# Later places in a state space branch's step loop, and other step rates, in a two-layer decoder trunk

## Chip, core and metric

The kernel runs on one core of one Trainium2 chip. The metric is device microseconds of one execution. A core has TensorE (PE, with its weight loads as PEld), VectorE (DVE), ScalarE (ACT), GpSimd (POOL) and SyncE (SP). Each works through its own row of instructions in the order in which they stand there. SP holds no arithmetic; its row is a queue of DMA issues.

## The reference, cut to what matters

A prompt of 2048 positions and a sample of 8x4 go through two layers of width 1024. Layer 0 is `proj = x @ w_in`, split into `u` (768), a gate (768), a memory query and a memory gate (256 each). Its mixer is a diagonal state space model (S5) of 48 groups with 16 channels and 64 complex states:

```
bu = einsum(ug, b_bar)                  # inputs of the states
h  = associative_scan(a*h + bu)         # over 2048 positions
y  = real(einsum(h, c)) + d_skip * ug
y  = gelu(y);  y = y * sigmoid(y @ w_glu + b_glu)      # the GLU
```

Beside it four heads attend from the memory query to 256 memory tokens. Both branches are gated, joined and projected by `w_out`, and a layer norm follows. Layer 1 (dilated attention) is untouched by the change.

## The kernel before

**Layer 0 in two streams.** The main stream is `run_units` (L228): weight columns of 128 times 1024 (or 1056) positions, in blocks of 512, 256 or 288 columns. Each block is 8 steps over the inner dimension, and each step three fp32r products (`mm3`, L128 to L130: high by high, low by high, high by low). So a block is 24 products into a PSUM tile `mm`, of which there are three. A block's end is taken out by ACT and DVE: for gate blocks ACT L290 (tanh) and then DVE L291, and a DMA stores `s` (L294). For every unit of weights ACT splits off the high part `wh` (L123) and DVE the low part `wl` (L124). When the units pass from the second half of the positions to the first, `XH` and `XL` are made anew from `xraw` in the same way.

**The side stream** is a Python generator. `tick` (L96) is called after every step of a block with that step's product time. It adds time x `self.rate` to a sum, and for each whole unit the generator does one more step. The rates stand in `self.R` (L73): `R[0]` for the first units, `R[1]` for the memory queries and gates of layer 0, `R[7]` for its memory attention, `R[2]` during the GLU.

**The S5 branch** (`s5`, L732) is that side stream. It works on 12 slices of four groups. For slice q a loop of 13 steps does:
- `tab_use` of q+1: products `aux` (L560) of tables `BS` and `E`, taken out by ACT as `kev` (L563) and stored in `d_kt`; then transposes of table `F` (L575), taken out by ACT as `I` (L577);
- `s5_out` of q-1: two steps, each with ten products `y` (L702 to L706; two of them read `H`, the states, and `E`), ACT's `Y` (L708), a POOL copy and two DMA stores (L712);
- `s5_scan` of q: DVE operations on `V` (L647 to L650), `C`, `f` (L682 to L684) and `H` (L688);
- `s5_load_t` of q+1: four DMAs that read `T` back from `d_kt` (L611);
- `s5_in` of q+1: eight products `v` (L627) from `U` and `I`, taken out by ACT as `V` (L630);
- `tab_make` of q+2: POOL makes `BA`, `BB`, `BS` from `bcraw` (loaded at L492), and DVE makes `F` and `E` (L507 to L511) and the small `CA`, `CB` (L546, L547).

`T`, `V`, `H` and `I` have two buffers each, `E` and `U` three, `CA` one; `aux` and `v` have one PSUM tile each, and so has a pair of `y`. A new writer waits for the last reader of its buffer.

**What sets the order.** The text's order is not yet the order on the engines. The program is built with `schedule_with_timeline_sim=True` (L2190): the builder places instructions by an estimate of its own of when operands are ready. Each engine then runs its row as placed.

After the S5 branch, memory attention (L901) is the side stream, first under the last gate blocks, then under the GLU (L1121), which begins when the last y is stored.

Of the kernel before, what the change touches and what calls it, by code (L numbers as in the profile page):

```python
# [48 lines left out]
class Tiles:  # L49


    def __init__(self, at):
        self.at = at
# [6 lines left out]
class Trunk:  # L60
    def __init__(self, tc, ins, outs):
        self.tc, self.nc, self.i, self.o = tc, tc.nc, ins, outs
        self.turn = 0
        self.bg = self.cache_copies()
        self.side, self.rate, self.acc = None, 0.0, 0.0
        self.bgrate, self.bgacc = 0.0, 0.0
        self.done = set()
        self.primed = None
        self.q2 = tc.nc.gpsimd

        self.B = (0.16, 0.0, 0.35, 0.056)

        self.R = (0.8, 0.9, 0.307, 0.34, 0.44, 0.51, 0.54, 0.48)  # L73

    def pool(self, name, bufs=1, space=None, side=None):
        kw = {"reuse_waits": "tile"}
# [655 lines left out]
    def s5(self, keep, d):  # L732

        nc = self.nc
        self.E, self.I, self.U, self.T, self.V, self.H = {}, {}, {}, {}, {}, {}
        self.F, self.BS, self.TR = {}, {}, {}
        with self.pool("tab", side="right") as tab, self.pool("aux", space=PSUM, side="right") as aux:
            self.ZR = tab.tile([128, 48], F32, name="ZR")
            self.ZI = tab.tile([128, 48], F32, name="ZI")
            self.ZRS = tab.tile([128, 48], F32, name="ZRS")  # L740
            self.ZIS = tab.tile([128, 48], F32, name="ZIS")
            for _ in range(12):
                yield
            with self.pool("base", side="right") as base:
                yield from self.s5_base(keep, tab, base)
            self.s5_setup(tab, d)
            self.tab_load(tab, 0)
            self.tab_load(tab, 1)
            yield
            yield from self.tab_make(tab, 0)  # L750
            yield
            yield from self.tab_use(tab, aux, 0, d)
            yield from self.tab_make(tab, 1)
            self.tab_load(tab, 2)
            yield from self.wait("u0")
            with self.pool("s5", side="right") as pool, self.pool("s5ps", space=PSUM, side="right") as psum:
                self.s5_load(pool, 0, d)
                self.s5_load_t(pool, 0, d)
                nc.sync.dma_start(self.H0S, self.i["h0_stack"])
                yield  # L760
                self.s5_in(pool, psum, 0)
                yield
                for q in range(NSL):


                    if q + 1 < NSL:
                        yield from self.wait(f"u{(q + 1) // 2}")
                    self.s5_load(pool, q + 1, d)
                    use = self.tab_use(tab, aux, q + 1, d)
                    make = self.tab_make(tab, q + 2)  # L770
                    out = self.s5_out(pool, psum, q - 1, d) if q else iter(())
                    scan = self.s5_scan(pool, q)
                    for n in range(13):
                        if n in (0, 3, 4):
                            next(use, None)
                        if n in (1, 2):
                            next(out, None)
                        if n < 9:
                            next(scan, None)
                        if n == 5:  # L780
                            self.s5_load_t(pool, q + 1, d)
                        if n == 9:
                            self.s5_in(pool, psum, q + 1)
                        if n >= 5 and n != 6:
                            next(make, None)
                        if n < 10 or q + 2 < NSL:
                            yield
                    self.tab_load(tab, q + 3)
                yield from self.s5_out(pool, psum, NSL - 1, d)
                self.s5_finish(pool, d)  # L790
# [1422 lines left out]
```

## Time and profile before

| | us |
|---|---|
| median of 3 runs | 1975.45 |
| lowest, highest | 1974.0, 1977.9 |
| the profiled execution, its own time | 1975.58 |
| its span, first to last instruction | 1973.8 |

The profiled execution's time is 1.78 us more than its span. The S5 branch runs from about 130 to 430 us of the span, memory attention of layer 0 from 479, the GLU from 552 to 700. Matmuls are pipelined: one of 512 columns shows 0.39 us, but they start 0.23 us apart, so PE is shown busy also where it just keeps pace; where it shows idle time it has certainly run dry.

### The profile page before, as it was taken

Reading aid. Unit: us, or ns where it says so; the run is one execution under the profiler, and the core shown is the slowest. Engines: PE = TensorE matmul, PEld = TensorE weight load, DVE = VectorE, ACT = ScalarE, POOL = GpSimd, SP = SyncE. Lnnn points to the kernel's source line nnn. Section 1 sums busy time; section 2 is a strip of 40 time slices with the busy share of each in tenths; the row PEclk is TensorE's granted clock in tenths of the full one; section 3 lists DMA queues with packets and bytes.
Section 4 is the critical chain, followed back from the end, with each engine's and each line's share of the span. In section 5 each row is a group of like instructions: output and inputs, shape, how many; then the busy total and the mean of one; then the engine's idle time right before and its main releaser. Section 6 shows DMA issues by size and latency. Waiting matters only on the chain.

```text
span 1973.8 us, 35795 instructions
## 1 busy us (share of the span) xinstructions
PE 1926.5 (98%) x13446; PEld 1643.7 (83%) x13446; DVE 1178.9 (60%) x2766; ACT 686.9 (35%) x1585; POOL 425.9 (22%) x754
## 2 busy tenths in 40 slices
PE   8999999899989999999999999999999999999998
PEld 6789888788779988787898879899888877887777
DVE  8649989885575756667456326532652245345685
ACT  5343222333453421115445226532652246221110
POOL 0414444313332012210000020003103210412220
PEclk9999999999999999999999999999999999999999
DMA  7685556656367899988533266536547736768941
GB/s 227 180 249 135 163 171 190 206 184 221 109 174 224 237 309 345 359 277 261 169 122 109 83 219 201 147 84 211 184 129 227 243 113 177 236 195 260 292 176 75
DMA packets 371893, 388.44 MB, mean 197 GB/s; under 512 B 76104, under 2 KB 314104, under 8 KB 369208
## 3 DMA queue, kind: packets, MB, share of 16 engines
q1 hardware_dynamic: 344904, 257.52, 43.7%
q0 software_dynamic: 26816, 128.63, 19.4%
q8 instruction: 106, 1.74, 0.4%
q14 instruction: 67, 0.55, 0.1%
HBM read 280.30 MB, written 150.27 MB: 218 GB/s over the span
## 4 chain that ended last, share of the span: by engine, by line
PE 83%; DMA 7%; DVE 5%; issue 1%; SPq 1%; ACT 1%; POOL 1%; DVEq 0%; ACTq 0%; POOLq 0%
PE mm L128 22%; PE mm L129 22%; PE mm L130 22%; PE s L1034 4%; PE o L1657 2%; PE tp L1642 2%; PE o L976 2%; PE tp L963 1%; DMA wraw<-in_w_in 1%; DMA bcraw<-in_ssm_bc 1%; DMA kv<-in_c_v 1%; PE tp L1389 1%; DVE wl L124 1%; DMA craw<-d_cm 1%; PE v L627 1%
## 5 line engine op out<-in xcount | busy, mean ns | idle before, releaser
L128 PE MATMUL mm<-XH,wh 128*128 128x512 f32 (+2 forms) x1520 | 546.7, 360 | 12.3 <-ACT wh L123 7.9
L129 PE MATMUL mm<-XH,wl 128*128 128x512 f32 (+2 forms) x1520 | 539.4, 355 | 1.0 <-DVE wl L124 1.0
L130 PE MATMUL mm<-XL,wh 128*128 128x512 f32 (+2 forms) x1520 | 538.2, 355 | 1.4 <-DVE XL L124 1.4
L128 PEld LDWEIGHTS mm<-XH,wh 128*128 128x128 f32 x1520 | 287.2, 189 | 60.6 <-ACT wh L123 8.5
L130 PEld LDWEIGHTS mm<-XL,wh 128*128 128x128 f32 x1520 | 287.1, 189 | 43.6 <-issue 3.0
L129 PEld LDWEIGHTS mm<-XH,wl 128*128 128x128 f32 x1520 | 286.8, 189 | 40.6 <-issue 2.4
L129 PE MATMUL mm<-WOH,cl 128*128 128x512 f32 (+1 forms) x512 | 197.5, 386 | 1.8 <-DVE cl L124 1.8
L128 PE MATMUL mm<-WOH,ch 128*128 128x512 f32 (+1 forms) x512 | 198.9, 390 | 0.1
L130 PE MATMUL mm<-WOL,ch 128*128 128x512 f32 (+1 forms) x512 | 197.8, 386 | 0.0
L124 DVE TENSOR_TENSOR wl<-wraw,wh 128x1024 fp32r<-128x1024 f32 (+1 forms) x87 | 103.5, 1190 | 52.9 <-ACT wh L123 51.6
L124 DVE TENSOR_TENSOR XL<-xraw,XH 128x512 fp32r<-128x512 f32 (+2 forms) x176 | 98.9, 594 | 36.6 <-ACT XH L123 35.3
L128 PE MATMUL mm<-v,XH 128*128 128x256 f32 (+1 forms) x408 | 118.3, 290 | 0.0
L129 PEld LDWEIGHTS mm<-WOH,cl 128*128 128x128 f32 x512 | 96.1, 188 | 23.7 <-DVE cl L124 3.4
L129 PE MATMUL mm<-v,XL 128*128 128x256 f32 (+1 forms) x408 | 115.5, 283 | 0.0
L130 PE MATMUL mm<-v,XH 128*128 128x256 f32 (+1 forms) x408 | 115.5, 283 | 0.0
L130 PEld LDWEIGHTS mm<-WOL,ch 128*128 128x128 f32 x512 | 96.1, 188 | 21.0
L128 PEld LDWEIGHTS mm<-WOH,ch 128*128 128x128 f32 x512 | 96.1, 188 | 20.5 <-ACT ch L123 0.5
L123 ACT ACTIVATE XH<-xraw 128x512 fp32r<-128x512 f32 (+2 forms) x176 | 91.7, 553 | 54.8 <-DMA xraw<-in_xT 18.5
L291 DVE SCALAR_TENSOR_TENSOR s<-s,mm 128x512 f32<-128x512 f32 (+2 forms) x80 | 46.7, 583 | 96.6 <-ACT s L290 90.7
L1631 ACT ACTIVATE P<-P,st 128x128 f32<-128x128 f32 (+1 forms) x192 | 86.1, 451 | 49.0 <-DVE st L1629 48.9
L123 ACT ACTIVATE wh<-wraw 128x1024 fp32r<-128x1024 f32 (+1 forms) x87 | 89.3, 1027 | 23.5 <-DMA wraw<-in_w_in 11.2
L1629 DVE CUSTOM_DVE_ANT_0 P<-s,NB 128x128 f32<-128x128 f32 (+1 forms) x192 | 58.6, 361 | 60.8 <-PE s L1034 60.7
(409 smaller groups left out, 3663.0 us busy)
## 6 DMA issues: line engine op xcount, KB each, us to landing
out_n_cache_dil_kv<-in_cache_dil_kv POOLq DMA_DIRECT2D x64, 512.0 KB, 6.1
wraw<-in_w_in SPq DMA_DIRECT2D x63, 512.0 KB
xraw<-d_x1TA SPq DMA_DIRECT2D x48, 256.0 KB
wraw<-in_w_kv SPq DMA_DIRECT2D x24, 512.0 KB
xraw<-in_xT SPq DMA_DIRECT2D x40, 256.0 KB
kv<-in_c_kT POOLq DMA_DIRECT2D x18, 512.0 KB, 6.3
kv<-in_c_v POOLq DMA_DIRECT2D x18, 512.0 KB, 5.7
xres<-in_x SPq DMA_DIRECT2D x16, 512.0 KB
```

Of the source, the lines that this page charges most:

```text
L123: self.nc.scalar.activation(hi, src, AF.Copy)
L124: self.nc.vector.tensor_tensor(lo, src, hi.bitcast(F32), op=OP.subtract)
L128: mm(out, wh, xh, start=first, stop=False)
L129: mm(out, wl, xh, start=False, stop=False)
L130: mm(out, wh, xl, start=False, stop=last)
L291: nc.vector.scalar_tensor_tensor(s[:, :n], s[:, :n], 1.0, p[:, :n], op0=OP.add, op1=OP.mult)
L976: mm(o[h * 64:h * 64 + 64, (t * 2 + y) * 128:(t * 2 + y) * 128 + 128], V[:, k, c:c + 64], pt[:, y, h, k], start=k == 0, stop=k == 1)
L1034: self.nc.tensor.matmul(s[:, h], a[pp, ts], b[pp, ks], start=n == 0, stop=n == 3, tile_position=(h * 64, 0))
L1629: v.tensor_tensor_reduce(out=P[:, h, y, lo:], in0=s[:, h, y, lo:], in1=NB[hp][:, h, lo:], scale=1.0, scalar=3e38, op0=OP.add, op1=OP.min, ...
L1631: nc.scalar.activation(P[:, h, y, lo:], P[:, h, y, lo:], AF.Exp, scale=-1.0, bias=at(0, hh, T + y), accum_out=at(1, hh, T + y))
L1642: nc.tensor.transpose(tp[:, h, k], P[:, h, y, k * 128:k * 128 + 128], ident)
L1657: mm(o[h * 64:h * 64 + 64, (t * 2 + y) * 128:(t * 2 + y) * 128 + 128], V[j][:, T + y - 1 + k - k0, h * 64:h * 64 + 64], pt[:, y, h, k], st ...
```

## The change

Two numbers in the table of rates: `R[1]` from 0.9 to 0.8 and `R[2]` from 0.307 to 0.38. In the loop of 13 steps, `s5_out` goes from steps 1 and 2 to steps 6 and 7, `s5_load_t` from step 5 to 8, and `s5_in` from step 9 to 10. Nothing is added or left out.

```
-        self.R = (0.8, 0.9, 0.307, 0.34, 0.44, 0.51, 0.54, 0.48)
+        self.R = (0.8, 0.8, 0.38, 0.34, 0.44, 0.51, 0.54, 0.48)
...
                     for n in range(13):
                         if n in (0, 3, 4):
                             next(use, None)
-                        if n in (1, 2):
+                        if n in (6, 7):
                             next(out, None)
                         if n < 9:
                             next(scan, None)
-                        if n == 5:
+                        if n == 8:
                             self.s5_load_t(pool, q + 1, d)
-                        if n == 9:
+                        if n == 10:
                             self.s5_in(pool, psum, q + 1)
                         if n >= 5 and n != 6:
                             next(make, None)
```

How this moves instructions is seen on ACT and DVE, whose rows hold one instruction for each end of a block. Take the seventh gate block, 256 columns wide. On ACT before, from the `V` of one slice to the `V` of the next (`Y` is the end of a pair of y products of the slice before, `kev` and `I` the ends of `aux`, `s<-mm` the end of a gate block):

```order
L630 ACTIVATE V<-v 64x2x136 x4
L708 ACTIVATE Y<-y 128x528
L290 ACTIVATE s<-mm 128x512
L563 ACTIVATE kev<-aux 128x256
L708 ACTIVATE Y<-y 128x528
L290 ACTIVATE s<-mm 128x288
L123 ACTIVATE wh<-wraw 128x1024
L577 ACTIVATE I<-aux 128x512
L290 ACTIVATE s<-mm 128x256
L577 ACTIVATE I<-aux 128x512
L290 ACTIVATE s<-mm 128x512
L630 ACTIVATE V<-v 64x2x136 x4
```

And on ACT now, from the same gate block on:

```order
L630 ACTIVATE V<-v 64x2x136 x4
L290 ACTIVATE s<-mm 128x512
L290 ACTIVATE s<-mm 128x288
L123 ACTIVATE wh<-wraw 128x1024
L290 ACTIVATE s<-mm 128x256
L563 ACTIVATE kev<-aux 128x256
L708 ACTIVATE Y<-y 128x528
L577 ACTIVATE I<-aux 128x512
L290 ACTIVATE s<-mm 128x512
L577 ACTIVATE I<-aux 128x512
L708 ACTIVATE Y<-y 128x528
L290 ACTIVATE s<-mm 128x288
```

The first `Y` has moved from right behind `V` to three gate blocks behind it; `kev`, both `I` and both `Y` now stand within one gate block's end of each other, where before they lay spread over four.

On DVE before, from the end of the seventh gate block (`s<-s,mm`) to the first `H` that follows it:

```order
L291 SCALAR_TENSOR_TENSOR s<-s,mm 128x256
L647 TENSOR_TENSOR s_3263<-C,CR 128x4x16
L648 TENSOR_TENSOR s_3264<-C,CS 128x4x16
L2015 COPY mark<-s 1x1
L649 TENSOR_TENSOR C<-C,s_3263 128x4x16
L650 TENSOR_TENSOR C<-C,s_3264 128x4x16
L546 TENSOR_SCALAR CA<-bcraw,sg 128x64
L682 TENSOR_TENSOR f_3303<-C,LR 128x256
L683 TENSOR_TENSOR f_3304<-C,LS 128x256
L684 TENSOR_TENSOR f_3303<-f_3303,f_3304 128x256
L688 TENSOR_TENSOR H<-V,f_3303 64x128 x4
```

On DVE now, two instructions behind the end of the same gate block:

```order
L688 TENSOR_TENSOR H<-V,f_3317 64x128 x4
L683 TENSOR_TENSOR f_3364<-C,LS 128x256
L682 TENSOR_TENSOR f_3363<-C,LR 128x256
L684 TENSOR_TENSOR f_3363<-f_3363,f_3364 128x256
L662 MEMSET C 128x4
L688 TENSOR_TENSOR H<-V,f_3363 64x128 x4
L507 TENSOR_TENSOR F<-P,BA 128x1024
L647 TENSOR_TENSOR s_3491<-V,LR 128x128
L648 TENSOR_TENSOR s_3492<-V,LS 128x128
L511 TENSOR_TENSOR F<-F,tT 128x1024
L546 TENSOR_SCALAR CA<-bcraw,sg 128x64
```

`H` stands behind the same gate block in both; `CA`, which reads the loaded `bcraw`, stood ahead of `H` and now stands behind it.

## Rows read from the trace of the kernel before

**Rows 1.** Windows: stretch, busy time and count by engine, granted clock, DMA share, GB/s.

```profile
core 0: us, PE busy (x) PEld busy (x) DVE busy (x) ACT busy (x) POOL busy (x), PEclk, DMA share, GB/s
225.00:430.00 205.00, 191.23 (x1257) 169.75 (x1257) 184.32 (x482) 63.37 (x118) 80.05 (x171) 0.98 0.60 184
280.00:290.00 10.00, 7.44 (x42) 6.69 (x41) 8.54 (x21) 2.75 (x6) 4.61 (x8) 0.83 0.47 147
360.00:370.00 10.00, 7.30 (x62) 7.09 (x61) 6.72 (x19) 3.54 (x7) 3.12 (x7) 1.00 0.47 138
390.00:400.00 10.00, 6.07 (x25) 4.80 (x24) 4.98 (x17) 3.58 (x7) 2.00 (x4) 0.85 0.85 269
```

**Rows 2.** PE's waits, 225 to 430 us: waiter, releaser, us in total, times, longest.

```profile
PE y L703 <- DVE H L688: 4.1, 2, 2.6
PE v L627 <- ACT I L577: 3.9, 1, 3.9
PE aux L560 <- DVE CB L547: 2.7, 2, 1.7
PE y L703 <- POOL VS L631: 2.7, 1, 2.7
PE aux L560 <- POOL BS L541: 0.3, 1, 0.3
```

**Rows 3.** DVE in order of time, 276 to 287 us: start, length, instruction, idle before.

```profile
278.57 0.23 DVE L650 TENSOR_TENSOR C<-C,s 128x64 f32<-128x64 f32 x1
...
281.12 0.39 DVE L546 TENSOR_SCALAR CA<-bcraw,sg 128x64 f32<-128x64 f32 x1 [2.32 <-DMA bcraw<-in_ssm_bc]
...
282.69 1.21 DVE L688 TENSOR_TENSOR H<-V,f 64x128 f32<-64x128 f32 x4
```

**Rows 4.** PE in order of time, 279 to 289 us.

```profile
280.48 0.39 PE L130 MATMUL mm<-XL,wh 128*128 128x512 f32 x1
283.42 0.47 PE L703 MATMUL y<-H,E 128*128 128x136 f32 x2 [2.56 <-DVE H L688]
```

**Rows 5.** SP's queue in order of time, 276 to 281 us.

```profile
277.36 0.58 SPq L492 DMA_DIRECT2D bcraw<-in_ssm_bc  x1
```

**Rows 6.** DVE in order of time, 359 to 366 us.

```profile
363.01 0.25 DVE L546 TENSOR_SCALAR CA<-bcraw,sg 128x64 f32<-128x64 f32 x1 [3.33 <-DMA bcraw<-in_ssm_bc]
363.18 0.52 DVE L684 TENSOR_TENSOR f<-f,f 128x256 f32<-128x256 f32 x1
363.73 1.21 DVE L688 TENSOR_TENSOR H<-V,f 64x128 f32<-64x128 f32 x4
```

**Rows 7.** PE in order of time, 360 to 366 us.

```profile
364.46 0.47 PE L703 MATMUL y<-H,E 128*128 128x136 f32 x2 [2.70 <-POOL VS L631]
```

**Rows 8.** DVE by line, 225 to 430 us: busy us, mean ns, idle before.

```profile
L124 DVE TENSOR_TENSOR XL<-xraw,XH 128x512 fp32r<-128x512 f32 x16 | 10.6, 687 | 5.6 <-ACT XH L123 5.6
L511 DVE TENSOR_TENSOR E<-E,tT 128x1088 f32<-128x1088 f32 x7 | 9.6, 1369 | 0.0
L546 DVE TENSOR_SCALAR CA<-bcraw,sg 128x64 f32<-128x64 f32 x5 | 1.4, 277 | 9.8 <-DMA bcraw<-in_ssm_bc 9.8
```

**Rows 9.** PE by line, the same stretch.

```profile
L128 PE MATMUL mm<-XH,wh 128*128 128x512 f32 (+2 forms) x250 | 86.9, 347 | 0.0
```

**Rows 10.** ACT by line, the same stretch.

```profile
L123 ACT ACTIVATE wh<-wraw 128x1024 fp32r<-128x1024 f32 x11 | 11.6, 1056 | 3.6 <-PE mm L130 3.6
...
L708 ACT ACTIVATE Y<-y 128x528 f32<-128x528 f32 x14 | 8.6, 612 | 37.5 <-issue 22.6 <-PE y L706 11.7 <-POOL BS L540 3.2
L577 ACT ACTIVATE I<-aux 128x512 f32<-128x512 f32 x14 | 8.3, 596 | 30.5 <-PE aux L575 30.5
L563 ACT ACTIVATE kev<-aux 128x256 f32<-128x256 f32 x7 | 2.7, 385 | 20.4 <-PE aux L560 20.3
```

**Rows 11.** ACT in order of time, 383 to 401 us.

```profile
395.22 0.63 ACT L123 ACTIVATE XH<-xraw 128x512 fp32r<-128x512 f32 x1 [5.63 <-DMA xraw<-in_xT]
395.76 0.58 ACT L577 ACTIVATE I<-aux 128x512 f32<-128x512 f32 x1
```

**Rows 12.** PE in order of time, 391 to 402 us.

```profile
396.39 1.49 PE L627 MATMUL v<-U,I 128*128 128x136 f32 x8 [3.93 <-ACT I L577]
```

More of the change, by code (lines that the diff above doesn't have):

```diff
@@ L71, in __init__ @@
         self.B = (0.16, 0.0, 0.35, 0.056)
-        self.R = (0.8, 0.9, 0.307, 0.34, 0.44, 0.51, 0.54, 0.48)
+        self.R = (0.8, 0.8, 0.38, 0.34, 0.44, 0.51, 0.54, 0.48)
     def pool(self, name, bufs=1, space=None, side=None):
@@ L775, in s5 @@
                             next(use, None)
-                        if n in (1, 2):
+                        if n in (6, 7):
                             next(out, None)
@@ L779, in s5 @@
                             next(scan, None)
-                        if n == 5:
+                        if n == 8:
                             self.s5_load_t(pool, q + 1, d)
-                        if n == 9:
+                        if n == 10:
                             self.s5_in(pool, psum, q + 1)
```

## The prediction, made before the change was run

> **What bounds the kernel now.** I read the windows first, since the change touches one stage, then the waits of PE there, then the instructions around each wait, and last the changed order.
>
> The stage is the S5 branch under the gate blocks. From 225 to 430 us PE shows 191.2 us busy of 205.0, so it ran dry for 13.8 us [rows 1]. The waits account for it: y products for `H` 4.1 and 2.7 us, the v products for `I` 3.9, `aux` for the tables 2.7 and 0.3, together 13.7 [rows 2]. To that comes the clock. In 280 to 290 us the granted clock is 0.83, in 390 to 400 it is 0.85 [rows 1]; between the levels 1.2 and 2.4 GHz this is 3.4 and 3.0 us at the low one, so 1.7 and 1.5 us of work lost. Both slices hold a long wait. The slice from 360 to 370 us holds one too, and its clock stays at 1.00 [rows 1]. So the stage loses about 17.0 us. Later stages stall too, but the order there does not change, as said below.
>
> What starts the y waits? SP issues `bcraw` at 277.36 us [rows 5]. DVE reaches `CA`, has nothing to read and sits for 2.32 us, until 281.12; `H` stands behind and comes at 282.69 [rows 3]. PE ends its last product before the wait at 280.48 plus 0.39 us and gets its y product off at 283.42, 2.56 us late [rows 4]. At 363 us it is the same: `CA` 3.33 us late, `H` from 363.73, the y product at 364.46, 2.70 us late [rows 6, 7]. The wait list names a POOL copy for that one [rows 2], but the first of four `H` had ended some 0.4 us before, so I count it as `H`. A late DMA thus reaches PE through DVE's row, because y stands close behind `H`.
>
> DVE is nearly as full as PE: 184.3 of 205.0 us, 20.7 idle [rows 1]. Of these 9.8 are `CA` waiting for `bcraw`, 5.6 `XL` waiting for `XH` [rows 8], and the remaining 5.3 small gaps.
>
> **The change, part by part.** The sum is made against the profiled execution's 1975.58 us, 0.13 above the median of the runs shown.
>
> Nothing is added, so busy time stays: 184.3 us of DVE work and 31 blocks of products (250 steps of eight each [rows 9]), or 6.6 us of the stage per block.
>
> *y five steps later.* `H` stays behind the same gate block. `Y`, the end of y, goes from right behind `V` to three gate blocks behind it, so y has some 20 us (3 x 6.6) more after its `H`. The longest wait to be covered is 2.7 us. I take all three off: 6.8 us, and the 1.7 us of clock behind the first. Value -8.5, bounds -8.5 and 0. What is late next is DVE itself, counted below. With the ten products go ACT's `Y`, a POOL copy and two stores for each pair; POOL is busy 80 of 205 us and can take it. On SP the stores now stand between the loads of `T`, two before and two behind them, since each `T` buffer is freed by these y products; behind them on SP wait the gate blocks' stores, `bcraw` and weights. The y products are old work by then, so I price this queue at nothing; if PE is late there, all of that list is.
>
> *`CA` behind `H`.* In the shown place `CA` now stands behind both `H` and two table operations. Its wait for `bcraw` no longer delays `H`, and I expect it to shrink, because more DVE work stands ahead of it: 9.8 to about 5 us.
>
> *aux.* The tables `E` of the next slice end some 2 blocks ahead of `aux` now; by my count of the order before, that was between 1 and 2, and both long `aux` waits stood where 10 us or more of DVE work lay behind one gate block. Of 3.0 us [rows 2] I take off 2.0; bounds -3.0 and 0. `E` has three buffers and its first operation (1.28 to 1.37 us each [rows 8]) must now wait for y of the slice three back, which ends only a block earlier; DVE tends to be behind PE, so I price that at nothing inside the DVE term.
>
> *The v wait at 396 us.* ACT held `I` behind an `XH` that waited 5.63 us for `xraw` [rows 11], and PE stood for 3.93 us [rows 12]. Now SP issues nine of those `xraw` loads ahead of the slice's `kev` store and `T` loads, where they were mixed. But `I` still stands behind most of the `XH`. I take half of 3.9 + 1.5: -2.7, bounds -5.4 and 0.
>
> *New waits on ACT.* `aux`, both transposes and both pairs of y now stand close together, so PE depends on ACT's `kev`, `I`, `Y` in quick turn, with a `wh` among them in some slices. No such wait shows in the trace of before. Bounds for each of eight slices: 0, and `wh` + `Y` + `I` in one row, 1.06 + 0.61 + 0.60 = 2.27 us [rows 10]. I take 0.4, near the lower end, as ACT is busy only 63 of 205 us [rows 1]: +3.2.
>
> *DVE as the bound.* These terms make -10.0, so the stage would be 195.0 us, with 10.7 us left for DVE's idle time. Its small gaps need 5.3; `CA` and `XL` would have to fall from 15.4 to 5.4, and I expect some 8 (5 and 3). The missing 2 to 3 us can in part be lateness that PE never feels, as `mm` has three tiles. I take +1.0; bounds 0 and +8.
>
> *Step rates.* A slice's 13 steps take 13/0.8 = 16.3 us of products instead of 14.4. But the builder places by readiness: after the last y product 231 rows of gate products stood before the first GLU product, and 227 do now. And from the first score on, PE's row of attention and GLU reads the same but for three or four products. So neither `R[1]` nor `R[2]` moves anything there that PE could feel: 0.
>
> Sum: -8.5 - 2.0 - 2.7 + 3.2 + 1.0 = -9.0, so 1975.58 - 9.0 = 1966.6 us.
>
> **The rivals.**
>
> *All waits go.* `XH` is in time, ACT costs nothing, DVE keeps up: -13.8 - 3.2 = -17.0, 1958.6 us. For it: seven waits have two causes, and both are moved. Against it: DVE would have 17 us less room with 20.7 us of idle time to place. 12 in 100.
>
> *DVE carries the stage.* If `CA` and `XL` keep their 15.4 us, DVE needs the full 205, whatever PE's order is, and the waits show up at `aux` or at block ends instead. PE can gain only by running ahead within its spare `mm` tile, at most a block (6.6 us), part of which it uses already; I take 2, 1973.6 us. For it: the S5 branch ends at the same gate block, so DVE gets no relief from slower steps. Against it: PE waits came one by one behind `CA`, and DVE was not full between them. 20 in 100.
>
> *Slower: PE waits for ACT in each cluster.* A transpose finds `I` behind `wh` and `Y`. The terms off are 13.2 us; over eight slices this rival decides from 13.2 / 8 = 1.65 us each. At 2.27 us it is 18.2 - 13.2 = +5.0, 1980.6 us. For it: ACT's row between `kev` and the second `I` holds a gate block's end that PE must first reach. Against it: of four slices only some have `wh` there. 12 in 100.
>
> *Clock.* Eight clusters with short waits could each cost what the wait at 283 us cost, 1.7 us, 13.6 in all: 1966.6 + 13.6 = 1980.2 us. The Trainium skill, "TensorE: Matmul & The Clock Gate", section "A second HAM failure mode: psum-queue depth-cycling", says that frequent short idle times between groups of matmuls alone can make the clock fall and rise again. By that rule this would be the outcome. The trace speaks against it, as even a wait of 2.70 us left the clock at 1.00 [rows 1, 7]. 4 in 100.
>
> **How the numbers follow.** The forecast, 1966.6, has 52 in 100 and by itself 1961 to 1972. A difference of 0.2%, 4.0 us, is about what a measurement of this kernel can tell from none. Faster by more: nearly all of the forecast (50), all waits gone (12), a part of DVE's case (4), 66 in 100. Within: 2 + 16 and 2 from the ACT case, 20. Slower: 10 + 4, 14. The range runs from 1957.5 to 1978: it takes in the first two rivals and leaves out the two slow ones and a little below.
>
> **What would show it.** Right: no y wait on `H` of over 0.5 us from 225 us on; `CA` waiting less than 9.8 us in total, with `H` not behind it; PE idle in the stage under 6 us; the clock at 1.00 around the old 283 us; DVE's busy time unchanged near 184 us, its share up; attention and GLU as long as before. Wrong: y, tr or v waits on ACT of over 1 us in most slices; `aux` waits grown to 6 us or more; the stage as long as before with DVE idle 20 us; or a stall at the passage to the GLU that the order does not show.

## The result and the profile after

The changed kernel takes 1961.18 us (median of 3 runs, 1960.28 to 1964.96) against 1975.45: a ratio of 0.9928, 95% interval 0.9915 to 0.9942, so 14.3 us less. The forecast was 1966.6, 9.0 us less, with a range of 1957.5 to 1978. The times of before differ by some us from chip to chip (its medians were 1975.45, 1978.55, 1979.84 and 1978.81 us), so the runs below are compared by their ratio to the kernel before in the same session. Where an expectation names a time, the ratio times 1975.45 is what answers to it.

The windows come first, as in [rows 1]. The profiled execution took 1961.18 us.

```profile
core 0: us, PE busy (x) PEld busy (x) DVE busy (x) ACT busy (x) POOL busy (x), PEclk, DMA share, GB/s
225.00:430.00 205.00, 203.88 (x1359) 182.38 (x1358) 194.65 (x511) 68.17 (x127) 78.10 (x178) 1.00 0.67 204
225.00:416.00 191.00, 189.88 (x1270) 169.81 (x1269) 184.53 (x483) 63.00 (x118) 75.41 (x172) 1.00 0.67 203
```

In the stretch of [rows 1] PE is now idle for 205.00 - 203.88 = 1.1 us, where it was idle for 13.8, and the clock is at 1.00 throughout. DVE does before's amount of work (483 instructions, 184.5 us) in 191 us instead of 205, at 97% of the time. PE's waits of the stretch, which answer to [rows 2]:

```profile
PE aux L560 <- DVE CB L547: 0.9, 1, 0.9
PE aux L560 <- DVE E L511: 0.2, 1, 0.2
```

No y product waits for `H`, no v product for `I`, and nothing waits for ACT. DVE by line answers to [rows 8]:

```profile
L124 DVE TENSOR_TENSOR XL<-xraw,XH 128x512 fp32r<-128x512 f32 x16 | 10.5, 702 | 0.0
L511 DVE TENSOR_TENSOR E<-E,tT 128x1088 f32<-128x1088 f32 x7 | 9.5, 1352 | 0.0
L546 DVE TENSOR_SCALAR CA<-bcraw,sg 128x64 f32<-128x64 f32 x6 | 1.5, 248 | 0.0
```

The columns behind the bars say it: `CA`, which waited 9.8 us for `bcraw`, and `XL`, which waited 5.6 us behind `XH`, wait no more. The operations themselves are as long as before. Two places show how. The first is SP and DVE around the `CA` that answers to [rows 3, 5]; first SP in order of time, 276 to 282 us:

```profile
276.88 1.23 SPq L611 DMA_DIRECT2D T<-d_kt  x2
278.15 0.97 SPq L712 DMA_DIRECT2D d_yT<-Y  x2
279.16 1.23 SPq L611 DMA_DIRECT2D T<-d_kt  x2
280.49 0.40 SPq L294 DMA_DIRECT2D d_gB<-s  x1
280.94 0.58 SPq L492 DMA_DIRECT2D bcraw<-in_ssm_bc  x1
```

and DVE, 282 to 288 us:

```profile
282.90 1.19 DVE L688 TENSOR_TENSOR H<-V,f 64x128 f32<-64x128 f32 x4
284.12 1.22 DVE L507 TENSOR_TENSOR F<-P,BA 128x1024 f32<-128x1024 f32 x1
285.26 0.38 DVE L647 TENSOR_TENSOR s<-V,LR 128x128 f32<-128x128 f32 x1
285.56 0.37 DVE L648 TENSOR_TENSOR s<-V,LS 128x128 f32<-128x128 f32 x1
285.85 1.21 DVE L511 TENSOR_TENSOR F<-F,tT 128x1024 f32<-128x1024 f32 x1
286.98 0.28 DVE L546 TENSOR_SCALAR CA<-bcraw,sg 128x64 f32<-128x64 f32 x1
```

`bcraw` is issued 280.94 and DVE comes to `CA` at 286.98: a lead of 6.0 us, and the bytes are there. Before, the lead was 281.12 - 2.32 - 277.36 = 1.4 us [rows 3, 5]. `H` stands ahead of `CA`. The second place is ACT, 376 to 386 us, which answers to [rows 11]:

```profile
379.86 0.59 ACT L577 ACTIVATE I<-aux 128x512 f32<-128x512 f32 x1
384.15 0.63 ACT L123 ACTIVATE XH<-xraw 128x512 fp32r<-128x512 f32 x1 [3.71 <-DMA xraw<-in_xT]
384.69 0.59 ACT L708 ACTIVATE Y<-y 128x528 f32<-128x528 f32 x1
385.18 0.59 ACT L577 ACTIVATE I<-aux 128x512 f32<-128x512 f32 x1
```

ACT still waits 3.71 us for `xraw`, with an `I` behind it, but the v products of that `I` were not due sooner: PE did not stop.

Where the 14.3 us come from: over the same 39 blocks of products, from the first product of one to the first product behind the last, it is 245.5 us before (169.6 to 415.1) and 228.5 after (172.4 to 400.9), so the stage gives 17.0, and 2.9 were lost ahead of it. One DVE operation, `CB`, that starts at 166.8 us before, starts at 169.8 after, where the order is still the same; in a second profile of the changed kernel (below) it starts at 167.4. So that loss is the execution's, not the change's.

### The profile page after: what moved, and what is told of

Same layout as the page of the kernel before. It is cut to its first block, busy times and chain, and to the rows that moved or that the text cites. A ratio compares the mean times of both kernels' runs of the same rounds, so it can differ in the third digit from the quotient of the medians.

```text
span 1959.3 us, 35798 instructions
## 1 busy us (share of the span) xinstructions
PE 1926.4 (98%) x13446; PEld 1645.6 (84%) x13446; DVE 1180.9 (60%) x2766; ACT 687.1 (35%) x1585; POOL 417.4 (21%) x754
## 4 chain that ended last, share of the span: by engine, by line
PE 84%; DVE 9%; DMA 4%; issue 2%; SPq 1%; ACT 1%; POOL 0%; DVEq 0%; ACTq 0%; POOLq 0%
PE mm L128 23%; PE mm L129 22%; PE mm L130 22%; PE s L1034 4%; PE o L1657 2%; PE tp L1642 2%; PE o L976 2%; PE tp L963 2%; DMA wraw<-in_w_in 1%; DVE wl L124 1%; DVE s L647 1%; DVE H L688 1%; PE tp L1389 1%; DVE tT L509 1%; DMA craw<-d_cm 1%
## 5 line engine op out<-in xcount | busy, mean ns | idle before, releaser
L290 ACT ACTIVATE s<-mm 128x512 f32<-128x512 f32 (+2 forms) x80 | 41.3, 516 | 156.9 <-PE mm L130 140.8
```

The costliest lines, as they stand in the source:

```text
L290: nc.scalar.activation(s[:, :n], p[:, :n], AF.Tanh, scale=0.5)
```

## Experiments

After the result I held two theories. *Distance*: PE waited because y stood close behind `H`; with more blocks between them PE no longer feels DVE's lateness. This is what the prediction said. *Transfer*: DVE is held at `CA` until `bcraw` lands, and PE waits for whatever stands behind `CA` on DVE, y or not; what counts is how long before `CA`'s turn `bcraw` is issued. Twelve runs followed, each beside the kernel before; one of them is the changed kernel again. "The rate" in them is `R[1]`; `R[2]` is 0.38 in every kernel made from the changed one and 0.307 in every kernel made from the one before. This table sums up their profiles in the window of [rows 1], 225 to 430 us: DVE's idle time before `CA` and before `XL`, PE's idle time (205 less its busy time) and the clock. The rows behind it follow where a verdict rests on them.

| kernel | CA + XL wait, us | PE idle, us | clock | ratio to before (95%) |
|---|---|---|---|---|
| before | 9.8 + 5.6 | 13.8 | 0.98 | 1 |
| y step alone | 9.0 + 6.3 | 13.7 | 0.98 | 1.0007 (0.9996 to 1.0017) |
| rate alone | 14.8 + 0.6 | 15.0 | 0.95 | 1.0041 (1.0028 to 1.0053) |
| load and input step alone | 12.2 + 6.5 | 13.2 | 0.96 | 0.9995 (0.9983 to 1.0008) |
| before, bcraw early | 0 + 6.0 | 5.2 | 0.98 | 0.9949 (0.9937 to 0.9961) |
| changed, y step back | 16.3 + 4.3 | 16.5 | 0.96 | 1.0010 (0.9996 to 1.0023) |
| changed, rate back | 9.2 + 7.1 | 14.7 | 0.98 | 0.9996 (0.9987 to 1.0006) |
| changed, bcraw late | 5.2 + 0.4 | 9.0 | 0.99 | 0.9971 (0.9960 to 0.9983) |
| changed, bcraw early | 0 + 6.3 | 6.7 | 0.98 | 0.9910 (0.9896 to 0.9924) |
| rate and y step | 0.8 + 6.4 | 8.4 | 0.98 | 0.9951 (0.9938 to 0.9965) |
| rate alone, bcraw early | 0 + 4.3 | 4.2 | 1.00 | 0.9958 (0.9946 to 0.9970) |
| changed, again | 2.6 + 0 | 3.5 | 0.99 | 0.9920 (0.9908 to 0.9933) |
| changed, first profile | 0 + 0 | 1.1 | 1.00 | 0.9928 (0.9915 to 0.9942) |
| changed, bcraw early, 7 xraw | 0 + 0 | 0.0 | 1.00 | 0.9859 (0.9843 to 0.9875) |

Read down, PE's idle time goes with DVE's wait for data: 13 to 17 us of the one where the other is 15 to 21, and 0 to 9 where it is 0 to 7. The distance of y does not sort them like that. From the end of the `H` that it reads to the first y product it is 0.1 to 1.2 us before (six slices of the window) and 0.8 to 1.8 in "before, bcraw early", whose PE idles 5.2 us; it is up to 7.5 and 9.4 us with the y step and with the rate alone, whose PE idles 14 and 15 us. Only the kernels with both have 10 us or more, and all of these lie at 9 us of idle time or below; for them the run with `bcraw` late is the test.

**The y step alone.**

```
-                        if n in (1, 2):
+                        if n in (6, 7):
                             next(out, None)
```

Expected: 

> The kernel before with one part of the change: the step that issues the y products stands at steps 6 and 7 of a slice, not 1 and 2; rates and the other two steps as before. In the order the y products then stand about 2 blocks of PE work behind their H, where they stood close behind it. Distance theory (the y products waited because they stood too close to H, and any two blocks cover what DVE loses): the seven long y waits go, -8.5 us by the prediction's term, so 1967 us, and 1961 us if the aux waits and the v wait go with them. Rate theory (only the slower rate of the branch gives DVE and the transfers their time): CA still waits 9.8 us for bcraw in sum, H is as late as before, and two blocks are not enough: 1971 to 1976 us. Transfer theory (the wait of CA for bcraw is the cause, wherever y stands): CA's wait stays near 9.8 us, and the time within 2 us of 1975.

Measured: no difference. PE's waits, 225 to 430 us:

```profile
PE aux L560 <- DVE CB L547: 8.0, 3, 5.2
PE aux L575 <- ACT I L577: 2.3, 1, 2.3
PE aux L560 <- DVE E L511: 2.2, 1, 2.2
PE mm L128 <- ACT XH L123: 0.6, 1, 0.6
PE y L703 <- DVE H L688: 0.6, 1, 0.6
```

y waits 0.6 us for `H` where it waited 4.1 (and 2.7 that I had counted with it) [rows 2]. But `aux`, whose table `E` is made from `CA` and `CB`, now waits 8.0. SP and then DVE at the longest one, 276 to 288 us:

```profile
277.65 2.48 SPq L611 DMA_DIRECT2D T<-d_kt  x4
281.19 0.51 SPq L294 DMA_DIRECT2D d_mg<-s  x1
281.74 0.59 SPq L492 DMA_DIRECT2D bcraw<-in_ssm_bc  x1
```

```profile
286.02 0.39 DVE L546 TENSOR_SCALAR CA<-bcraw,sg 128x64 f32<-128x64 f32 x1 [5.14 <-DMA bcraw<-in_ssm_bc]
```

DVE is at `CA` at 286.02 - 5.14 = 280.88 us, 0.9 us before `bcraw` is even issued. The distance does what it should to y, and it gains nothing: the next reader of the same late engine takes over the wait.

**The rate alone.**

```
-        self.R = (0.8, 0.9, 0.307, 0.34, 0.44, 0.51, 0.54, 0.48)
+        self.R = (0.8, 0.8, 0.307, 0.34, 0.44, 0.51, 0.54, 0.48)
```

Expected: 

> The kernel before with one number changed: the rate of the state space branch is 0.8 in place of 0.9; no step is moved. In the order the y products then stand about 2 blocks behind their H as well, because the whole branch is spaced wider. Rate theory: all of the stage's 17.0 us go, 1959 to 1962 us, and CA's waits for bcraw fall below 2 us in sum. Distance theory: the same as with the moved y step alone, 1961 to 1967 us. If the moved steps were what counts: within 2 us of 1975.

Measured: 0.4% slower, which no theory expected. PE's waits, 225 to 430 us, and DVE's line for `CA`:

```profile
PE aux L560 <- DVE CB L547: 10.9, 2, 6.5
PE aux L560 <- POOL BS L541: 4.2, 1, 4.2
```

```profile
L546 DVE TENSOR_SCALAR CA<-bcraw,sg 128x64 f32<-128x64 f32 x6 | 1.9, 314 | 14.8 <-DMA bcraw<-in_ssm_bc 14.8
```

All of PE's idle time hangs on `bcraw`, through DVE and, for `BS`, through POOL. Outside the stage this order pays too: one product of the output projection waits 3.9 us for its split context (`ch`) where before shows no such wait. The other runs say where it comes from: it is 4.5 us in the one other kernel with `R[1]` at 0.8 and `R[2]` at 0.307 (below), and 0.4 to 0.9 us in the seven profiles with `R[1]` at 0.8 and `R[2]` at 0.38. So the rate alone costs there, and the higher `R[2]` goes with its absence; a run with `R[2]` alone was not made.

**The load and the input step alone.**

```
-                        if n == 5:
+                        if n == 8:
                             self.s5_load_t(pool, q + 1, d)
-                        if n == 9:
+                        if n == 10:
                             self.s5_in(pool, psum, q + 1)
```

Expected: 

> The kernel before with the two other moves alone: the load of the next slice's weights at step 8 (was 5) and its input products at step 10 (was 9). The order of PE is nearly that of the kernel before. Distance and rate theory: within 0.2% of 1975 us, 17 us lost in the stage as before. Transfer theory (the later load leaves the queue to bcraw and xraw): the CA waits and the 5.6 us wait of XH shrink, and the time falls by 5 us or more, to 1970 us or below.

Measured: no difference, with much the waits of before (`CA` 12.2 us). So the transfer theory in the form I gave it there (that the place of the `T` loads alone delays `bcraw`) falls.

**The kernel before with `bcraw` loaded one slice earlier.**

```
-        raw = pool.tile([128, 4, GS, 16], F32, name="bcraw", bufs=2)
+        raw = pool.tile([128, 4, GS, 16], F32, name="bcraw", bufs=3)
...
-                    self.tab_load(tab, q + 3)
+                    self.tab_load(tab, q + 4)
```

(`dd` gets three buffers too, and slice 3 is loaded ahead of the loop.)

Expected: 

> The kernel before with bcraw and dd loaded one slice of d earlier, into three buffers in place of two; steps and rates as before, so that the y products stay as close behind H as in the kernel before. Transfer theory: CA no longer waits (9.8 us in sum before, below 1 now), H comes in time, and the y waits go: 1967 us or less. Distance theory: CA's wait goes, but the y products stand so close that DVE's own pace still makes them wait 0.5 to 1.5 us at most of the eight places: 1969 to 1975 us. If H was late through DVE's other work and not through CA: within 2 us of 1975.

Measured: 0.9949, 10 us less (1965.4 by the ratio). PE's waits, 225 to 430 us, are down to

```profile
PE v L627 <- ACT I L577: 3.7, 1, 3.7
PE aux L560 <- DVE CB L547: 1.5, 3, 0.6
```

and y stands as close to `H` as ever. DVE, then PE, 278 to 282 us:

```profile
278.22 1.21 DVE L688 TENSOR_TENSOR H<-V,f 64x128 f32<-64x128 f32 x4
280.71 1.21 DVE L688 TENSOR_TENSOR H<-V,f 64x128 f32<-64x128 f32 x4
```

```profile
280.29 0.39 PE L703 MATMUL y<-H,E 128*128 128x136 f32 x2
281.42 0.39 PE L703 MATMUL y<-H,E 128*128 128x136 f32 x2
```

The y product starts 0.9 us after the end of the `H` it reads (278.22 + 1.21) and has not waited. The y waits were the transfer's, then, and no step had to move to remove them. What is left is the v wait. So 10 us of the change's 14 to 16 can be had by the early load alone.

**The changed kernel with one part put back**, the y step (`if n in (1, 2)`) or the rate (`R[1]` at 0.9, with `R[2]` left at 0.38).

Expected, y step back: 

> The changed kernel with the y products back at steps 1 and 2; rates and the other two moves as changed. y stands about 2 blocks of PE work behind H here, 3.5 to 4 in the changed kernel. Transfer theory as the first four runs left it (PE waits wherever DVE is held at CA until bcraw lands; whether it is held is set by how long before CA's turn bcraw is issued): the rate alone gave CA waits of 14.8 us and 1985 us, so this, which differs from it by the two small moves, comes out near it, 1975 to 1986 us, with CA waits over 8 us. Distance theory (two to four blocks between H and y are what matters): 1961 to 1967 us.

Expected, rate back: 

> The changed kernel with the branch's rate back at 0.9; all three moves of steps as changed. Transfer theory: like the run with the y step alone moved, whose branch has the same spacing: CA waits of about 9 us, PE waits at aux in place of y, 1974 to 1981 us. Distance theory: 1961 to 1967 us. If both come out at 1974 or more here and with the y step put back, the gain needs the two parts together and is no sum of theirs.

Measured: 1.0010 and 0.9996, both as the transfer theory had it. (The first differs from the rate alone by `R[2]` too, and not by the two small moves only, as I wrote.) PE's waits in each, the two largest lines:

```profile
PE aux L560 <- DVE CB L547: 13.5, 3, 6.0
PE v L627 <- ACT I L577: 1.3, 1, 1.3
```

```profile
PE aux L560 <- DVE CB L547: 7.9, 3, 5.2
PE v L627 <- ACT I L577: 2.4, 1, 2.4
```

The gain is no sum of the parts: either one put back takes away all of it.

**The changed kernel with `bcraw` loaded later.**

```
                             self.s5_load_t(pool, q + 1, d)
+                        if n == 4 and q:
+                            self.tab_load(tab, q + 2)
...
-                    self.tab_load(tab, q + 3)
```

Expected: 

> The changed kernel with bcraw and dd of slice q+2 loaded at step 4 of slice q in place of the end of slice q-1: five of thirteen steps later, about 9 us of a slice's 24. In the changed kernel 3.7 to 6.7 us lie between bcraw's issue and CA's turn. Transfer theory: CA waits again, 2 to 6 us in most of six slices, 10 to 35 us in sum, PE takes half or more of that at aux, and the time is 1972 to 1990 us although y still stands 3 or more blocks behind H. Distance theory: within 2 us of the changed kernel's 1961 us.

Measured: 0.9971, so some 60% of the changed kernel's gain is gone. By the ratio that is 1969.7 us, between the two theories: less than the 1972 I set for the transfer theory, and far from the 1961 of the other, though y starts 12 to 15 us after its `H`. The `CA` waits came to 5.2 us, half of the least I expected, since the order put `CA` later as well. PE waits 2.7 us for `CB` and 3.5 for `E`, with y far behind `H`.

**The changed kernel with `bcraw` loaded earlier**, by the edit above.

Expected: 

> The changed kernel with bcraw and dd loaded one slice earlier, into three buffers. The order of PE is that of the changed kernel. Transfer theory: CA has no wait there that could still go, so the time is the changed kernel's within 2 us, 1959 to 1963 us; with 1967 us of the kernel before given the same early load, what is left of the change beyond bcraw is then 4 to 8 us (there the v wait of 3.7 us, 1.5 us of aux and the clock at 0.98). If POOL's waits for bcraw (16.9 us in sum in the changed kernel) also cost time: 1955 to 1959 us.

Measured: 1960.38 us, 0.9910, so 1957.7 by the ratio; the intervals of this and of the changed kernel overlap. That is what `CA` with no wait left to lose would give, but it lies in the range that I had set for POOL's waits costing time, so whether they cost a few us is not settled. Against the early load in the kernel before (0.9949) it is clearly less, by some 8 us, with no y wait in either; where these come from is not shown. The profiled execution took 1965.65 us, 5.3 more than the median of the six. In its profile the one wait over 1 us left in the stage is the v wait: SP had issued the last `xraw` by 377.95 us, and ACT gets it at 387.31. ACT, then PE, 376 to 390 us:

```profile
387.31 0.63 ACT L123 ACTIVATE XH<-xraw 128x512 fp32r<-128x512 f32 x1 [10.00 <-DMA xraw<-in_xT]
388.33 0.59 ACT L577 ACTIVATE I<-aux 128x512 f32<-128x512 f32 x1
```

```profile
388.97 2.13 PE L627 MATMUL v<-U,I 128*128 128x136 f32 x8 [6.12 <-ACT I L577]
```

That is the second wait of the same kind: ACT held at `XH` by a transfer, `I` behind it, PE behind `I`. With 6.1 us it is about what that execution lies above the median, so the others may not have had it.

**Rate and y step without the two small moves.**

Expected: 

> The changed kernel with the load step back at 5 and the input step back at 9: what is left is the rate of 0.8 (with the later memory attention) and the y products at steps 6 and 7. The order of PE differs from the changed kernel's in 233 lines of some 10,000, and bcraw stands in SP's queue at like places, behind a store and not straight behind the four T loads. Transfer theory: no or little CA wait, 1959 to 1965 us, so that the rate and the y step suffice together although each alone gave nothing. If the two small moves are needed as well: 1972 us or more, with CA waits over 5 us.

Measured: 0.9951, 1965.8 us by the ratio, just above the first of the two cases I had set. `CA` waits 0.8 us in sum, so these two parts do bring `bcraw` in time. But ACT waited 10.18 us for an `xraw` at 391 us, and PE with it:

```profile
PE mm L128 <- ACT XH L123: 5.3, 1, 5.3
PE mm L128 <- DVE s L291: 1.7, 2, 1.1
```

SP issued that `xraw` at 383.76 us, 2.4 us after ACT's turn at it; in the two profiles of the changed kernel the same load is issued at 379.38 and 379.54, and ACT waits 3.7 and 3.4 us without PE stopping. This fits two transfers sharing the change's gain: with `bcraw` in time and `xraw` late it is 0.9949 (before, `bcraw` early) and 0.9951 (here), with both in time 0.9928 and 0.9920. Whether the two small moves are what brings `xraw` in time is open: the two kernels with one part put back have them, and `XL` waits 4.3 and 7.1 us there. No run moved `xraw` by itself.

**The rate alone, with `bcraw` early.**

Expected: 

> The kernel before with the rate of 0.8, which alone came out at 1985 us with 14.8 us of CA waits, and bcraw loaded one slice earlier. Transfer theory: the CA waits go and with them the whole of PE's 15 us at aux: 1960 to 1968 us, though y stands where it stood in that run. If the slower rate costs by itself (POOL's wait of 4.2 us, the spacing): 1972 us or more.

Measured: 0.9958, 1967.2 us by the ratio, at the upper end of what I expected. The stage did what the theory says: PE idle went from 15.0 to 4.2 us. But the output projection's wait for `ch` stayed (4.5 us here, 3.9 with the rate alone).

**The changed kernel again.**

Expected: 

> The changed kernel once more, beside the others on the same chip: 0.993 of the kernel before, and again no CA wait over 1 us and no y wait on H in its stage. If bcraw's landing was luck of one execution, CA waits of some us come back.

Measured: 0.9920. The `CA` waits came to 2.6 us in this profile, more than the 1 us I allowed, and `aux` waited 2.6 for `E`: so the landing does vary from one execution to the next. The `CA` that waited longest came 4.1 us after the issue of its `bcraw` and waited 1.95; in the first profile it came 4.0 after and did not wait. The change has brought the loads in time with little to spare.

**A version that beats both:** the changed kernel with `bcraw` early, and seven `xraw` buffers (`self.nraw = 7`, was 6).

Expected: 

> A try at a version that beats both: the changed kernel with bcraw loaded one slice earlier, and seven buffers of xraw in place of six, so that the pieces of x for which XH waited 6.3 us (and the v products behind it 6.1 us) are asked for sooner. If XH's wait goes and nothing else moves: 6 us less than the run with bcraw early, 1954 to 1957 us. If the new buffer only shifts the order and the transfers (it changes the order of most of the program): 1958 to 1970 us.

Measured: 1951.3 us, 0.9859 (0.9843 to 0.9875), clearly below the changed kernel on the same chip (0.9920). Its window:

```profile
225.00:430.00 205.00, 204.96 (x1357) 183.20 (x1356) 196.21 (x519) 69.15 (x128) 79.66 (x175) 1.00 0.66 198
```

PE is idle for 0.04 us of 205; no wait is listed. That is more than the 6 us of the v wait: at the first gate blocks, in the GLU and in the output projection PE is further ahead too, which I did not take apart.

## Why the prediction was right, and where its sizes were off

*Direction and place: right.* The stage lost its stalls and the granted clock its dips, nothing else was touched; the sign is the one with 66 in 100. The signs named for "right" are all in the first profile: no y wait on `H`, `CA` below 9.8 us, PE idle under 6 us, clock at 1.00, DVE's work unchanged, the GLU as long as before (148.8 and 149.6 us from its first split to its last tanh). But these signs do not tell a gain from the distance of y from one by the landing of `bcraw`, and the direction was in part luck: the two parts that I had priced by themselves, the y step and the rate, give 1.0007 and 1.0041 by themselves.

*The -8.5 for y: right number, wrong reason.* The step that failed is that distance would cover the lateness of DVE. The 20 us were too many: y starts 10.6 to 15.2 us after its `H` in the changed kernel, up to 7.5 with the y step alone. Alone it took the y waits from 6.8 to 0.6 us as I had it, and the time stayed at 1.0007, since `aux` took the wait over. The y waits go just as well with y where it was, once `bcraw` comes early (0.9949). The rows had shown the chain from `bcraw` to y [rows 3, 6], and I took the last link for the cause. To count the wait at 364 us as one for `H`, against the list, was right: y starts 0.15 us after the second of the four `H` ends, at 364.32, just as it does at 283 us (283.28, 283.42). That `CA` moved behind `H` was no gain either: with `bcraw` late, `aux` waits instead.

*Step rates 0: the step that failed.* I compared the order of PE after the branch and found it alike. The rate works inside the branch: together with the y step it sets where `bcraw` stands in SP's queue and `CA` in DVE's, and so the lead of the one over the other. At the place shown at 280 us that lead is 1.4 us before, -0.9 with the y step alone, -1.1 with the rate alone and 6.0 with both. Without the rate, nothing is left (0.9996). Nor is it nothing behind the branch: with `R[1]` lowered alone PE waits 3.9 us at `ch`, and with `R[2]` raised as well 0.4 to 0.9, so the two rates hang together there.

*DVE as the bound, +1.0, and `CA` and `XL` at 8: too cautious.* Both went to 0. DVE then works through at 97%, and PE hardly waits: 0 instead of +1.0. The rival in which DVE carries the stage had its condition, `CA` and `XL` keeping their 15.4 us, met in the runs with one part only, and they do come out at 1974 us or more; in the changed kernel the condition is not met.

*v, -2.7 of -5.4; aux, -2.0 of -3.0; ACT, +3.2.* v went off wholly; 1.1 us are left at `aux`, so -1.9; no wait on ACT came, so the 8 x 0.4 were 0. Put together: -8.5 - 1.9 - 5.4 is -15.8, with the rest of the 17.0 in the clock and small stalls. So in the stage the first rival, all waits go, was nearest (1958.6 us); 2.9 us of that execution were lost ahead of the stage. The v wait went although ACT still waited 3.71 us for the last `xraw`; the early `bcraw` by itself had left it at 3.7 us. On another chip the ratio was 0.9920, 15.8 us of 1978.81.

*The clock rival.* The clusters of short waits that it needs did not appear, so the rule cited from the Trainium skill could not act here and is not tested. The stretch showed a clock of 0.95 and 0.96 with 14.8 and 16.3 us of `CA` waits, and 0.98 to 1.00 with none.

What stays open: why the same transfer lands after 4 us in one place and 7 in another; what brings `xraw` in time in the changed kernel, and so the last 4 to 6 us of its gain; what `R[2]` does by itself, which was not tried.

## What to carry to other kernels

When an engine in the middle is held by a transfer, look at the first wait of the chain, not at the last: moving the reader away hands the wait to the next reader, loading earlier removes it. Compare the time of a load's issue with the time at which the engine comes to its first reader; here a lead of 1.4 us was too short, one of 4 us sometimes (363.01 - 3.33 - 355.52 = 4.2 us, and 3.3 too few, before; 4.0 at the same load in the changed kernel, and enough), one of a whole slice never. Where a builder sets the order from such steps, their effects need not add up: try the parts apart, and do the direct thing (one more buffer) before tuning steps.

## What the runs showed of the hardware

The same 128 KB load of `bcraw` took 2.6 to 7.5 us from issue to use by a waiting DVE around the stage of the kernel before, and up to 8.1 in the other runs. Two cases of the kernel before, both behind `T` loads on SP: issued at 277.36, `CA` at 281.12, 3.8 us [rows 3, 5]; and, SP in order of time, 353 to 356 us,

```profile
353.00 2.48 SPq L611 DMA_DIRECT2D T<-d_kt  x4
355.52 0.58 SPq L492 DMA_DIRECT2D bcraw<-in_ssm_bc  x1
```

with `CA` at 363.01 [rows 6], 7.5 us. The DMA engines' busy share was 0.79 from 277 to 281 us and 0.92 from 355 to 363:

```profile
355.00:363.00 8.00, 6.76 (x48) 6.14 (x46) 4.30 (x18) 2.77 (x6) 0.65 (x2) 1.00 0.92 284
277.00:281.00 4.00, 3.87 (x22) 3.00 (x20) 1.77 (x8) 1.00 (x3) 0.66 (x2) 1.00 0.79 221
```

Of these two the busier stretch has the slower landing, but a third case of the same kernel does not fit: issued at 248.13 behind `T` loads, used at 255.51, 7.4 us, with the engines less busy.

```profile
248.13:255.51 7.38, 7.38 (x61) 7.24 (x60) 5.22 (x19) 3.71 (x8) 0.00 (x0) 1.00 0.72 232
```

So the busy share does not order the landings. The Trainium skill, "DMA: Bandwidth & Descriptors", section "Issuing engines are not separate DMA queues", says that all transfers run on the same 16 DMA engines and interleave, whichever engine issued them; no run here shows it, since none held one load apart.
